# Two-stream DeepNorm backbone on one core: where the second half's scaling stands in ScalarE's queue

## The chip, the core and the metric

The kernel runs on one core of a Trainium2 chip. The metric is the device time of one execution in microseconds (us). The engines work side by side, each through its own queue in order: TensorE (PE in the rows, PEld for its weight loads), VectorE (DVE), ScalarE (ACT), GpSimd (POOL) and SyncE (SP), whose queue issues nearly all transfers here. An instruction at the head of a queue that waits for a semaphore holds up all that stands behind it in that queue.

## What is computed

Two layers run over 256 latent tokens (two row tiles of 128) with 1024 features; in the first layer 256 context tokens (two more row tiles) run through the same weights up to the attention. Each layer is a feed-forward block, a token mixer (attention in layer 0, a short gated convolution in layer 1) and a second feed-forward block. Each of these reads a modulated input and ends in a layer norm:

```python
def modulate(x, shift, scale):
    return x * (1 + scale) + shift

def post_norm_update(x, y, gate, res_w, g, b):
    return layer_norm(DN_ALPHA * x + res_w * gate * y, g, b)

def swiglu_ffn(h, w_in, w_out):
    a, u = jnp.split(h @ w_in, 2, axis=-1)
    return (jax.nn.silu(a) * u) @ w_out

def half_step_ffn(x, shift, scale, gate, w_in, w_out, g, b):
    y = swiglu_ffn(modulate(x, shift, scale), w_in, w_out)
    return post_norm_update(x, y, gate, 0.5, g, b)
```

## The kernel before

Every matmul is done in three parts on numbers split in two: `split` (L108) has ScalarE write a rounded "hi" copy (L110), and VectorE write the rest, "lo" = value - hi (L111). Weights are split in the same way as they come in: SyncE loads a raw tile (`wunit`, L203), ScalarE makes hi in two halves (L208), VectorE lo in two halves (L211). `mmu` then issues hi x hi (L162), lo x hi (L163) and hi x lo (L165). Four raw weight tiles exist, so a load is issued when the lo copies of the tile four loads earlier are through.

The function that the change touches is `modulated` (L408). It is called 12 times, once for each row tile at the end of each block that has a follower: four tiles after the first feed-forward block, and two tiles each after the attention, the second feed-forward block, the first block of layer 1 and the convolution. It normalizes the tile on VectorE (L411, which waits for a small GpSimd step, L400 and L401, behind the statistics of L398). Later it does for each half h of the 1024 features: four 128x128 transposes on TensorE into one PSUM bank (L419), four scalings of 128x128 on ScalarE that apply the modulation and the norm's gain (L425), then the hi copy (L110, tile hTh) and the lo copy (L111, tile hTl). The matmuls of the next block take the first half's hTh and hTl for their first two weight units (k = 0 to 3) and the second half's for the next two.

TensorE's order is written out by hand. For the other engines a scheduler lays out the order when the program is built: among the instructions that it reckons to be ready it takes them by priority, and `tc.high_priority` moves a block ahead. `queued(ins)` (L373) adds an order: instructions of the block come behind the given ones in the same engine's queue. A moved instruction on one engine can therefore change the order of others, SP's transfers among them.

Other names in the steps below: `roped` (L856 to L863) rotates queries and keys on VectorE, and L939 transposes the queries on TensorE; `gated` makes the gate (`sil`, L476 on ScalarE, L477 on VectorE), which TensorE transposes a little later (L485); `new_x` (L778, L779) multiplies x by the norm's gain `lng` and adds `lnb`, which SP loads just before (L343).

Of the kernel before, what the change touches and what calls it, by code (L numbers as in the profile page):

```python
# [11 lines left out]
AF = mybir.ActivationFunctionType  # L12
# [4 lines left out]
P = 128  # L17
# [51 lines left out]
def backbone_kernel(  # L69
# [6 lines left out]
    nc = tc.nc  # L76
# [16 lines left out]
    def nm(s):  # L93
        uid[0] += 1
        return f"{s}_{uid[0]}"

    def act(dt=F32, s="a"):
        return ap.tile([P, 512], dt, tag="act", name=nm(s))
# [7 lines left out]
    def tpb(s="tp"):  # L106
        return bank("tp", s)

    def split(src, hi, lo):
        a = nc.scalar.activation(hi, src, AF.Copy)  # L110
        return a, nc.vector.tensor_tensor(out=lo, in0=src, in1=hi.bitcast(F32), op=ALU.subtract)  # L111
# [261 lines left out]
    def queued(ins):  # L373

        es = ExitStack()
        for i in ins:
            es.enter_context(tc.issue_after(i.ins))
        return es
# [29 lines left out]
    def modulated(z, mv, rs, GB, lag, ahead=False):  # L408

        for h in range(2):  # L410
            norm_ins[1:] = [nc.vector.tensor_scalar(z[h], z[h], mv[:, 0:1], rs, op0=ALU.subtract, op1=ALU.mult)]  # L411

        def rest():
            G, B = GB.get()
            res = []
            for h in range(2):
                ps = tpb("hT")
                for k in range(4):
                    nc.tensor.transpose(ps[:, k * P:(k + 1) * P], z[h][:, k * P:(k + 1) * P], ident)  # L419
                t = sp.tile([P, 512], F32, tag="s2", bufs=S2, name=nm("h"))  # L420
                with tc.high_priority(offset=LN_EARLY):
                    hi, lo = act(F32R, "hTh"), act(F32R, "hTl")
                    for k in range(4):
                        s, c = slice(k * P, (k + 1) * P), slice(4 * h + k, 4 * h + k + 1)
                        nc.scalar.activation(t[:, s], ps[:, s], AF.Identity, bias=B[:, c], scale=G[:, c])  # L425
                    ins = split(t, hi, lo)
                res.append((hi, lo))
            if ahead:
                fence[:] = [i.ins for i in ins]
            return res  # L430

        return Late(lag, rest)
# [266 lines left out]
    for q, (k0, n) in enumerate(steps):  # L699
        nxt = start_step(*steps[q + 1]) if q < 4 else iter(())  # L700
        for g in range(6 * n):
            for _ in range(NS[min(q, 2)][g]):
                next(nxt, 0)
            k = k0 + g // 6
# [517 lines left out]
```

## Time and profile before

| | |
|---|---|
| median of 3 runs | 1264.56 us (1263.3 to 1265.16) |
| the profiled execution | 1262.04 us, of which the span of the core is 1260.2 us |
| granted TensorE clock | 0.999 of full speed |
| TensorE matmul busy | 1242.7 us, 99% of the span |
| TensorE weight loads busy | 1004.2 us, 80% |
| VectorE busy | 950.1 us, 75% |
| ScalarE busy | 589.2 us, 47% |
| GpSimd busy | 41.5 us, 3% |

Times in the trace are counted from the start of the span. The profiled execution took 1262.04 us, 2.5 us less than the median of the runs. In the rows of a timeline the first number is the start, the second the time from there to the end of the last instruction that is merged into the row, and a bracket at the end gives the idle time of that engine before the row and what ended it.

### The profile page before, as it was taken

The numbers are of one execution on the slowest core, as the hardware profiler recorded it, in microseconds if no ns is written. First come the engines' busy times: TensorE is split into PE (matmuls) and PEld (weight loads), VectorE is DVE, ScalarE is ACT, GpSimd is POOL, SyncE is SP. The second block draws the span as 40 slices with busy tenths as digits, with TensorE's granted clock in tenths as the row PEclk, the third lists the DMA queues.
The fourth block names the chain that finished last, engine by engine and source line by source line (L and its number), as shares of the span: only waits on it lengthen the run. The fifth ranks groups of instructions, "written<-read, shape, count | busy, mean of one in ns | idle before, by whom it ended". The sixth has DMA issues, their size and how long they took to land.

```text
span 1260.2 us, 17282 instructions
## 1 busy us (share of the span) xinstructions
PE 1242.7 (99%) x5910; PEld 1004.2 (80%) x5910; DVE 950.1 (75%) x1678; ACT 589.2 (47%) x1152; POOL 41.5 (3%) x71
## 2 busy tenths in 40 slices
PE   8999999999999999989999999999999999999997
PEld 5787778777878877867888788888788887888786
DVE  3699987888868877789889546988546788976546
ACT  2432132312326456687655435655435744655431
POOL 0000000000001111121000000000000000000000
PEclk9999999999999999999999999999999999999999
DMA  9976678788842744464899645898645764886641
GB/s 308 299 240 220 197 241 291 254 269 281 284 137 85 218 92 92 93 148 147 263 321 338 221 146 168 278 341 275 213 146 170 245 204 131 270 282 184 228 152 55
DMA packets 202776, 268.59 MB, mean 213 GB/s; under 512 B 30090, under 2 KB 149362, under 8 KB 202688
## 3 DMA queue, kind: packets, MB, share of 16 engines
q1 hardware_dynamic: 202652, 267.48, 67.2%
q8 instruction: 46, 0.75, 0.2%
q14 instruction: 42, 0.34, 0.1%
q10 hardware_dynamic: 36, 0.02, 0.0%
HBM read 265.27 MB, written 2.17 MB: 212 GB/s over the span
## 4 chain that ended last, share of the span: by engine, by line
PE 90%; ACT 3%; DVE 3%; DMA 2%; issue 1%; SPq 0%; POOL 0%; DVEq 0%; ACTq 0%
PE f L677 19%; PE w L162 17%; PE w L165 17%; PE w L163 17%; PE wkv L162 2%; PE wkv L163 2%; PE wkv L165 2%; PE wc L162 2%; PE wc L165 2%; PE wc L163 2%; PE gT L485 1%; DMA ar<-in_ada_w_dram 1%; PE ada L325 1%; PE hT L419 1%; PE S L962 1%
## 5 line engine op out<-in xcount | busy, mean ns | idle before, releaser
L208 ACT ACTIVATE w1h<-w1r 128x512 fp32r<-128x512 f32 (+1 forms) x352 | 199.9, 620 | 183.6 <-DMA w1r<-in_ffn_w_in_dram 63.5
L211 DVE TENSOR_TENSOR w1l<-w1r,w1h 128x512 fp32r<-128x512 f32 (+1 forms) x352 | 222.8, 678 | 49.2 <-ACT w1h L208 47.6
L162 PE MATMUL w<-w1h,hTh 128*128 128x512 f32 x528 | 209.4, 397 | 0.9 <-ACT hTh L110 0.9
L163 PE MATMUL w<-w1l,hTh 128*128 128x512 f32 x528 | 206.0, 390 | 0.2 <-DVE w1l L211 0.2
L294 DVE SCALAR_TENSOR_TENSOR acc<-ar,cst,acc 128x512 f32<-128x512 f32 x266 | 186.0, 745 | 14.5 <-DMA ar<-in_ada_w_dram 14.3
L162 PE MATMUL w<-w2h,gh 128*128 128x512 f32 (+1 forms) x446 | 173.4, 389 | 0.0
L163 PE MATMUL w<-w2l,gh 128*128 128x512 f32 (+1 forms) x446 | 172.1, 386 | 0.0
L211 DVE TENSOR_TENSOR w2l<-w2r,w2h 128x512 fp32r<-128x512 f32 x176 | 114.3, 687 | 76.3 <-ACT w2h L208 75.5
L208 ACT ACTIVATE w2h<-w2r 128x512 fp32r<-128x512 f32 x176 | 101.6, 624 | 145.4 <-PE w L165 101.6
L165 PE MATMUL w<-w1h,hTl 128*128 128x512 f32 x528 | 163.2, 390 | 0.3 <-DVE hTl L111 0.2
L165 PE MATMUL w<-w2h,gl 128*128 128x512 f32 (+1 forms) x446 | 136.0, 386 | 0.0
L677 PE MATMUL f<-h0h,w1h 128*128 128x512 f32 x352 | 132.8, 393 | 1.0 <-ACT w1h L208 0.6
L677 PE MATMUL f<-h0l,w1h 128*128 128x512 f32 x352 | 133.2, 391 | 0.0
L677 PE MATMUL f<-h0h,w1l 128*128 128x512 f32 x352 | 132.7, 390 | 0.0
L162 PEld LDWEIGHTS w<-w1h,hTh 128*128 128x128 f32 x528 | 99.2, 188 | 23.8 <-ACT hTh L110 1.7
L165 PEld LDWEIGHTS w<-w1h,hTl 128*128 128x128 f32 x528 | 98.9, 188 | 22.4 <-DVE hTl L111 1.5
L163 PEld LDWEIGHTS w<-w1l,hTh 128*128 128x128 f32 x528 | 99.2, 188 | 20.2 <-DVE w1l L211 0.6
L162 PEld LDWEIGHTS w<-w2h,gh 128*128 128x128 f32 x446 | 83.8, 188 | 19.3 <-issue 1.7
L163 PEld LDWEIGHTS w<-w2l,gh 128*128 128x128 f32 x446 | 83.8, 188 | 16.5
L165 PEld LDWEIGHTS w<-w2h,gl 128*128 128x128 f32 x446 | 83.3, 188 | 17.1
L677 PEld LDWEIGHTS f<-h0h,w1h 128*128 128x128 f32 x352 | 65.5, 188 | 19.4 <-issue 4.2
L677 PEld LDWEIGHTS f<-h0l,w1h 128*128 128x128 f32 x352 | 65.6, 188 | 14.3 <-issue 1.0
(184 smaller groups left out, 1697.3 us busy)
## 6 DMA issues: line engine op xcount, KB each, us to landing
w1r<-in_ffn_w_in_dram SPq DMA_DIRECT2D x340, 256.0 KB
ar<-in_ada_w_dram SPq DMA_DIRECT2D x128, 512.0 KB
w2r<-in_ffn_w_out_dram SPq DMA_DIRECT2D x88, 512.0 KB
ar<-in_ada_w_dram SPq DMA_DIRECT2D x32, 256.0 KB
wkvr<-in_na_w_qkv_dram SPq DMA_DIRECT2D x32, 256.0 KB
wcr<-in_sc_w_in_dram SPq DMA_DIRECT2D x32, 256.0 KB
wqr<-in_na_w_qkv_dram SPq DMA_DIRECT2D x8, 512.0 KB
bias<-in_na_rpb_dram SPq DMA_DIRECT2D x64, 64.0 KB
```

The costliest lines, as they stand in the source:

```text
L162: nc.tensor.matmul(ps, lh, rh, start=first and i == 0, stop=False)
L163: nc.tensor.matmul(ps, lh, rl, start=False, stop=False)
L165: nc.tensor.matmul(ps, ll, rh, start=False, stop=last and i == n - 1)
L208: nc.scalar.activation(hi[:, a:a + m // W_HI], raw[:, a:a + m // W_HI], AF.Copy)
L211: nc.vector.tensor_tensor(out=lo[:, a:b], in0=raw[:, a:b], in1=hi[:, a:b].bitcast(F32), op=ALU.subtract)
L294: nc.vector.scalar_tensor_tensor(out=a, in0=src, scalar=sc, in1=a, op0=ALU.mult, op1=ALU.add)
L325: nc.tensor.matmul(ps[32 * j:32 * j + 32, :], ones, acc[i][h], start=True, stop=True)
L419: nc.tensor.transpose(ps[:, k * P:(k + 1) * P], z[h][:, k * P:(k + 1) * P], ident)
L485: nc.tensor.transpose(ps[:, j * 256 + i * P:j * 256 + (i + 1) * P], g[:, j * P:(j + 1) * P], ident)
L677: nc.tensor.matmul(ps, w, hT0[k][part == 1], start=(k == part == 0), stop=(k == KC - 1 and part == 1))
L962: nc.tensor.matmul(banks[i], (qh, qh, ql)[f][ps, qs], (kh, kl, kh)[f][ps, :], start=f == 0, stop=f == 2)
```

## The change

In `modulated`, the four scalings of the second half (h = 1) are put behind the first half's hi copy (`ins[0]`) in ScalarE's queue. Nothing is added, removed or resized; no number changes.

```diff
                     hi, lo = act(F32R, "hTh"), act(F32R, "hTl")
-                    for k in range(4):
-                        s, c = slice(k * P, (k + 1) * P), slice(4 * h + k, 4 * h + k + 1)
-                        nc.scalar.activation(t[:, s], ps[:, s], AF.Identity, bias=B[:, c], scale=G[:, c])
+                    with queued([ins[0]] if h else ()):
+                        for k in range(4):
+                            s, c = slice(k * P, (k + 1) * P), slice(4 * h + k, 4 * h + k + 1)
+                            nc.scalar.activation(t[:, s], ps[:, s], AF.Identity, bias=B[:, c], scale=G[:, c])
                     ins = split(t, hi, lo)
```

In all 12 calls the order before is: four scalings of the first half, one of the second, hi copy of the first, three scalings of the second, hi copy of the second. TensorE's and GpSimd's orders stay as they are; ScalarE's changes in all 12 calls, and VectorE's and SP's around some of them. Line numbers of the changed kernel are one higher from L423 on.

**After the attention, first row tile.** ScalarE before, where `h_5702` and `h_5716` are the scaled halves, `hTh_5703` and `hTh_5717` their hi copies, and `w1h_5760` the hi copy of the third weight unit of the next block:

```order
L208 ACTIVATE w1h_5760<-w1r_5759 128x512
L425 ACTIVATE h_5702<-hT_5697,gcol_5490 128x128 x4
L425 ACTIVATE h_5716<-hT_5711,gcol_5490 128x128
L110 ACTIVATE hTh_5703<-h_5702 128x512
L425 ACTIVATE h_5716<-hT_5711,gcol_5490 128x128 x3
L208 ACTIVATE w1h_5760<-w1r_5759 128x512
L110 ACTIVATE hTh_5717<-h_5716 128x512
```

and ScalarE now:

```order
L208 ACTIVATE w1h_5760<-w1r_5759 128x512
L426 ACTIVATE h_5702<-hT_5697,gcol_5490 128x128 x4
L208 ACTIVATE w1h_5760<-w1r_5759 128x512
L110 ACTIVATE hTh_5703<-h_5702 128x512
L426 ACTIVATE h_5716<-hT_5711,gcol_5490 128x128 x4
L110 ACTIVATE hTh_5717<-h_5716 128x512
```

The place of the fifth scaling ahead of the first hi copy is taken by a weight copy of 128x512, which stood ahead of the second hi copy. (In the other calls nothing takes that place, except for the fourth tile of the first block and the second tile here, where it is a weight copy too.)

VectorE at the same place before, with `w1l_5761` and `w1l_5776` the lo copies of the third and fourth weight units, `st`, `mv` and `rs` the statistics of the second row tile:

```order
L111 TENSOR_TENSOR hTl_5704<-h_5702,hTh_5703 128x512
L389 SCALAR_TENSOR_TENSOR x_5241<-x_5241,res_5731 128x512
L211 TENSOR_TENSOR w1l_5776<-w1r_5774,w1h_5775 128x512
L111 TENSOR_TENSOR hTl_5718<-h_5716,hTh_5717 128x512
L391 BN_STATS st_5673<-x_5241 128x6
L211 TENSOR_TENSOR w1l_5761<-w1r_5759,w1h_5760 128x512
L398 BN_AGGR mv_5735<-st_5673 128x2
L211 TENSOR_TENSOR w1l_5776<-w1r_5774,w1h_5775 128x512
L411 TENSOR_SCALAR x_5239<-x_5239,mv_5735,rs_5737 128x512
L411 TENSOR_SCALAR x_5241<-x_5241,mv_5735,rs_5737 128x512
```

and VectorE now:

```order
L111 TENSOR_TENSOR hTl_5704<-h_5702,hTh_5703 128x512
L389 SCALAR_TENSOR_TENSOR x_5241<-x_5241,res_5731 128x512
L211 TENSOR_TENSOR w1l_5761<-w1r_5759,w1h_5760 128x512
L391 BN_STATS st_5673<-x_5241 128x6
L111 TENSOR_TENSOR hTl_5718<-h_5716,hTh_5717 128x512
L398 BN_AGGR mv_5735<-st_5673 128x2
L211 TENSOR_TENSOR w1l_5776<-w1r_5774,w1h_5775 128x512
L411 TENSOR_SCALAR x_5239<-x_5239,mv_5735,rs_5737 128x512
L411 TENSOR_SCALAR x_5241<-x_5241,mv_5735,rs_5737 128x512
L211 TENSOR_TENSOR w1l_5776<-w1r_5774,w1h_5775 128x512
```

The second half of `w1l_5761` moves ahead; the second half of `w1l_5776` moves behind the two L411, which wait for GpSimd.

**At the start of the attention.** VectorE before, with `qr_3652` the rotated queries of the second row tile (`r_621` its scratch) and `wkvl` the lo copies of key and value weights:

```order
L211 TENSOR_TENSOR wkvl_3709<-wkvr_3707,wkvh_3708 128x512
L111 TENSOR_TENSOR hTl_3619<-h_3617,hTh_3618 128x512
L856 TENSOR_TENSOR qr_3652<-wq_3599,rope 128x512
L861 TENSOR_TENSOR r_621_3653<-wq_3599,rope 128x16x16 x2
L111 TENSOR_TENSOR hTl_3633<-h_3631,hTh_3632 128x512
L863 TENSOR_TENSOR qr_3652<-qr_3652,r_621_3653 128x512
```

and VectorE now:

```order
L211 TENSOR_TENSOR wkvl_3709<-wkvr_3707,wkvh_3708 128x512 x2
L111 TENSOR_TENSOR hTl_3619<-h_3617,hTh_3618 128x512
L857 TENSOR_TENSOR qr_3652<-wq_3599,rope 128x512
L862 TENSOR_TENSOR r_621_3653<-wq_3599,rope 128x16x16 x2
L211 TENSOR_TENSOR wkvl_3724<-wkvr_3722,wkvh_3723 128x512
L864 TENSOR_TENSOR qr_3652<-qr_3652,r_621_3653 128x512
```

One more weight copy stands ahead of the row tile's rotation, and ahead of its last step there is a weight copy where `hTl_3633` stood.

**After the second feed-forward block of layer 0, second row tile.** VectorE before, with `w1l_7689` a lo copy of the next block's weights and `hTl_7553` the lo copy of the first half:

```order
L211 TENSOR_TENSOR w1l_7659<-w1r_7657,w1h_7658 128x512 x2
L211 TENSOR_TENSOR w1l_7689<-w1r_7687,w1h_7688 128x512 x2
L111 TENSOR_TENSOR hTl_7553<-h_7551,hTh_7552 128x512
L292 TENSOR_SCALAR acc_7622<-ar_7574,cst 128x512 x2
L111 TENSOR_TENSOR hTl_7567<-h_7565,hTh_7566 128x512
```

and VectorE now:

```order
L211 TENSOR_TENSOR w1l_7659<-w1r_7657,w1h_7658 128x512 x2
L211 TENSOR_TENSOR w1l_7689<-w1r_7687,w1h_7688 128x512
L111 TENSOR_TENSOR hTl_7553<-h_7551,hTh_7552 128x512
L211 TENSOR_TENSOR w1l_7689<-w1r_7687,w1h_7688 128x512
L292 TENSOR_SCALAR acc_7622<-ar_7574,cst 128x512 x2
L111 TENSOR_TENSOR hTl_7567<-h_7565,hTh_7566 128x512
```

`hTl_7553` now stands one weight copy earlier.

On SP some transfers change places. The one that the text below speaks of is in the second feed-forward block of layer 0: before, the four loads of `lng` and `lnb` for `new_x` stood ahead of the two loads of the weight tile `w1r_6151`; now the first of those two stands ahead of them. VectorE's order there has the first L778 (which needs `lng`) directly behind the gate of the first row tile and ahead of the gate of the second, before and now.

## Rows read from the trace of the kernel before

**Rows 1.** The page: busy time by engine, and the chain's shares by engine.
```profile
PE 1242.7 (99%) x5910; PEld 1004.2 (80%) x5910; DVE 950.1 (75%) x1678; ACT 589.2 (47%) x1152; POOL 41.5 (3%) x71
...
PE 90%; ACT 3%; DVE 3%; DMA 2%; issue 1%; SPq 0%; POOL 0%; DVEq 0%; ACTq 0%
```
**Rows 2.** Waits of PE, whole span: us in total, times, longest.
```profile
PE w L162 <- ACT hTh L110: 0.9, 2, 0.7
...
PE w L165 <- DVE hTl L111: 0.2, 1, 0.2
```
**Rows 3.** Timeline of ACT after the convolution, first row tile.
```profile
1062.83 1.85 ACT L425 ACTIVATE h<-hT,gcol 128x128 f32<-128x128 f32 x5 [2.01 <-PE hT L419]
1064.56 0.64 ACT L110 ACTIVATE hTh<-h 128x512 fp32r<-128x512 f32 x1
1065.08 1.17 ACT L425 ACTIVATE h<-hT,gcol 128x128 f32<-128x128 f32 x3
1066.28 0.63 ACT L110 ACTIVATE hTh<-h 128x512 fp32r<-128x512 f32 x1
```
**Rows 4.** Timelines of DVE and PE after the convolution, second row tile.
```profile
1074.70 0.68 DVE L111 TENSOR_TENSOR hTl<-h,hTh 128x512 fp32r<-128x512 f32 x1
...
1075.44 0.73 PE L165 MATMUL w<-w1h,hTl 128*128 128x512 f32 x2
```
**Rows 5.** Timeline of ACT after the attention, first row tile.
```profile
589.91 1.85 ACT L425 ACTIVATE h<-hT,gcol 128x128 f32<-128x128 f32 x5
591.63 0.65 ACT L110 ACTIVATE hTh<-h 128x512 fp32r<-128x512 f32 x1
```
**Rows 6.** Timeline of DVE at the same place.
```profile
592.86 0.67 DVE L111 TENSOR_TENSOR hTl<-h,hTh 128x512 fp32r<-128x512 f32 x1
...
596.47 0.19 DVE L398 BATCH_NORM_AGGREGATE mv<-st 128x2 f32<-128x12 f32 x1
...
597.93 1.00 DVE L411 TENSOR_SCALAR x<-x,mv,rs 128x512 f32<-128x512 f32 x2 [0.72 <-POOL rs L401]
598.85 1.28 DVE L211 TENSOR_TENSOR w1l<-w1r,w1h 128x512 fp32r<-128x512 f32 x2
```
**Rows 7.** Timeline of PE at the same place.
```profile
596.59 0.50 PE L163 MATMUL w<-w1l,hTh 128*128 128x512 f32 x1 [0.19 <-DVE w1l L211]
...
597.86 0.39 PE L162 MATMUL w<-w1h,hTh 128*128 128x512 f32 x1
598.08 0.39 PE L163 MATMUL w<-w1l,hTh 128*128 128x512 f32 x1
```
**Rows 8.** Timelines of DVE and PEld at the start of the attention.
```profile
412.03 0.69 DVE L863 TENSOR_TENSOR qr<-qr,r 128x512 f32<-128x512 f32 x1
...
412.77 0.75 PEld L939 LDWEIGHTS qT<-ident,qr 128*128 128x128 f32 x7 [0.32 <-DVE qr L863]
```
**Rows 9.** Timelines of DVE and PE after layer 0's second block, second row tile.
```profile
791.47 0.68 DVE L111 TENSOR_TENSOR hTl<-h,hTh 128x512 fp32r<-128x512 f32 x1
...
791.60 0.39 PE L163 MATMUL w<-w1l,hTh 128*128 128x512 f32 x1
792.21 0.73 PE L165 MATMUL w<-w1h,hTl 128*128 128x512 f32 x2 [0.21 <-DVE hTl L111]
```
**Rows 10.** Timelines of SP, DVE and PEld around `new_x`, layer 0, second block.
```profile
612.08 0.94 SPq L343 DMA_DIRECT2D lng<-in_ln_g_dram  x2
...
614.60 11.63 SPq L203 DMA_DIRECT2D w1r<-in_ffn_w_in_dram  x8
...
618.26 0.68 DVE L778 TENSOR_TENSOR x<-x,lng 128x512 f32<-128x512 f32 x1
...
620.35 0.58 PEld L485 LDWEIGHTS gT<-ident,sil 128*128 128x128 f32 x4
```
**Rows 11.** Timelines of SP and DVE around `new_x`, layer 1, first block.
```profile
801.49 0.93 SPq L343 DMA_DIRECT2D lng<-in_ln_g_dram  x2
...
807.47 1.29 DVE L778 TENSOR_TENSOR x<-x,lng 128x512 f32<-128x512 f32 x2 [1.21 <-DMA lng<-in_ln_g_dram]
```

## The prediction

> **What bounds the kernel now.** I read the page first, then TensorE's waits over the whole span, then the timelines of ScalarE, VectorE, TensorE and SyncE around each of the 12 calls of `modulated`. TensorE is busy 1242.7 of 1260.2 us and has 90% of the chain that ended last [rows 1]. All that TensorE does not do in the span is 17.5 us, so a change that leaves its work alone can gain only out of that. The change touches the hi copies of the modulated input, and for them TensorE waits 0.9 us in two places, and 0.2 us for a lo copy [rows 2]. The reader is to see there that the direct stake is about 1 us of 1260, and that whatever else the change does, it does through the order in which ScalarE, VectorE and SyncE now stand.
>
> The sum is made against the profiled execution: 1262.04 us with a span of 1260.2 us. The median of the runs shown is 1264.56 us, 2.52 us above; I add that difference at the end.
>
> **Part 1, the copy itself.** In a call the five scalings start 0.35 us apart: five of them take 1.85 us and one alone some 0.46 [rows 3]. The first hi copy starts 1.73 us after the first scaling, though its own four are through after 3 x 0.35 + 0.46 = 1.51 us. In the second half the copy starts 0.03 us after its last scaling has ended (1065.08 + 1.17 = 1066.25, copy at 1066.28) [rows 3]. So with nothing in between the first copy would start at about 1.54 us: 0.19 earlier. The second copy gets four scalings behind the first copy in place of three, so it comes 0.35 - 0.19 = 0.16 later. Nine of the 12 calls go this way. In the other three a weight copy slips into the gap, which takes 0.52 us of the queue (1064.56 to 1065.08 for a copy of that size [rows 3]) in place of 0.35, and the first hi copy comes 0.17 later.
>
> What that is worth at TensorE: the 0.7 us wait [rows 2] is the one after the convolution, where the first copy ends at 1065.20 [rows 3]. It would shrink by 0.19. But nine microseconds on, TensorE waits for the second row tile's lo copy, which VectorE ends at 1074.70 + 0.68 = 1075.38, with the matmul at 1075.44 [rows 4]; VectorE works without a gap up to there and starts nothing earlier. The 0.19 is lost again: 0, with 0 to -0.19 as bounds. The 0.2 us wait is the one after the attention. There a weight copy slips in, so the first copy starts at 589.91 + 4 x 0.35 + 0.52 = 591.82 instead of 591.63 [rows 5] and ends at 592.47. TensorE starts 0.19 later, but the first matmul with the lo half waits for VectorE, which reaches that copy at 592.86 as before [rows 6], so nothing is left of it: 0. The second halves are first needed two weight units later, 2.7 us at 12 matmuls of 0.22 to 0.23 us [rows 7]; a copy that is 0.16 later costs nothing.
>
> A rule of the Trainium skill speaks against this change: in the page Perfetto Trace Analysis, section "Optimizing Scalar/DVE Operations", half of a ScalarE instruction's profiled latency is write acknowledgement that overlaps with the next instruction, so an independent instruction between a producer and its reader is a cover, and the change removes one in each call. The trace agrees: the copy that stands directly behind its scaling starts 0.50 us after that scaling's start (1065.08 + 2 x 0.35 = 1065.78), where 0.35 would do [rows 3]. By the rows the exposed 0.15 us falls on ScalarE, busy 47% [rows 1], and is worth 0; by the rule alone, if all 12 lay on the path, the sum would have 12 x 0.15 = 1.8 us more (rival C).
>
> **Part 2, VectorE after the attention.** Here the scheduler now places the second half of the fourth weight unit's lo copy (`w1l_5776`) behind the two L411, which wait for GpSimd. VectorE's slots are 0.60 us (two in 1.28, one 0.68 [rows 6]). From the lo copy at 592.86: L389 593.46, `w1l_5761` 594.06, statistics 594.67, second lo copy 595.27, L398 at 595.87, which is one slot earlier than 596.47. From L398 to L411 it is 1.46 us [rows 6], so L411 starts at 597.33. The pair takes 0.92 (597.93 to 598.85 [rows 6]), so the delayed copy runs from 598.25 to 598.92. TensorE wants it at 598.08 [rows 7], and before that gets back the 0.35 us stall at 596.59, because `w1l_5761` is now early. It can start at about 598.98: **+0.90 us**. From there on every wait in the trace hangs on TensorE's own progress or has slack, so it stays. If GpSimd's step were 0.3 us faster it would be +0.6; that is the lower bound. The upper bound is +0.9, since the copy's time does not depend on TensorE.
>
> **Part 3, VectorE at the start of the attention.** The query transposes wait for the last step of the second row tile's rotation, L863 at 412.03, which ends at 412.72; the weight load goes at 412.77 after a wait of 0.32 [rows 8]. Now one weight copy more stands ahead of the rotation (the lo copy before it moves too, and some of VectorE's idle time there goes, so I reckon +0.5 us for its start), and ahead of L863 a weight copy replaces a lo copy of the same length. L863 comes at about 412.45: **+0.45 us**. Bounds 0.4 to 0.5 if it stays; attention has other waits of TensorE that could take it back, so the lower bound is 0.
>
> **Part 4, VectorE after layer 0's second block.** The lo copy at 791.47 holds TensorE: matmuls follow each other by 0.22 to 0.23 us, so after 791.60 the next was due at 791.83, started at 792.21, and its slot was 0.11 longer (0.73 in place of 0.62 for two) [rows 9]. The copy now stands one slot of 0.60 earlier and ends at 791.55: **-0.49 us**. Lower gain 0.2, if the gate a few microseconds on becomes the next wait.
>
> All else that moves in the queues (weight copies that trade places with gate copies, `lng` ahead of half a weight load) lies beside TensorE's work with several microseconds to spare: 0.
>
> **Sum.** 0 + 0.90 + 0.45 - 0.49 = +0.86 us: profiled 1262.9, span 1261.1, and with the 2.52 us of the median 1265.4 us. With the bounds of the parts: -0.19 + 0.6 + 0 - 0.49 = -0.1 to 0 + 0.9 + 0.5 - 0.2 = +1.2, 1264.5 to 1265.8. The runs of before lie 1.9 us apart, so a median may sit 0.9 us to either side.
>
> **Rival A, slower: `lng` comes late.** In layer 0's second block SyncE now issues one load of a weight tile ahead of `lng`. That load waits for a raw tile to come free, which was so at 614.60 [rows 10] and will be some 0.75 us later, as VectorE there runs later. `lng` is then issued at about 615.8 instead of 612.08. If it takes 5.9 us, as from 801.49 to about 807.4 [rows 11], it lands at 621.7. L778 stood at 618.26 without a wait, and behind it, 0.6 us on, the gate of the second row tile, which TensorE's transposes take from 620.35 [rows 10]. With the 0.9 us of part 2 TensorE comes at 621.25; the gate would be through at 621.7 + 0.6 + 0.4 = 622.7: a stall of 1.45 us. Against it: the loads issued ahead should have drained by then, and `lng` may land within 3 to 4 us. It decides from a landing after 620.3. With the parts at their upper bounds: 1.2 + 1.45 = +2.65, 1267.2 us, slower by 0.21%; with the forecast's parts 1266.9.
>
> **Rival B, the gains alone.** VectorE's new orders cost nothing (GpSimd's step or the scaling earlier than reckoned, or attention takes it back), and TensorE keeps the 0.19 and the 0.49: -0.7 us, 1263.9. For it: parts 2 and 3 rest on slots that I counted out, not on rows of the new order, and 0.9 us is less than two slots. Against it: at 598.08 TensorE has no slack that a copy behind L411 could use.
>
> **Rival C, the second copy sits on the path.** The rule of part 1: 12 x 0.15 = 1.8 us on top of the sum, +2.7 and 1267.2 us. Against it: the 2.7 us until the second half is needed.
>
> **How the numbers follow.** Forecast 0.62, A 0.18, B 0.16, C 0.04. 0.2% is 2.5 us, about what a measurement of this kernel can tell from no change: faster means under 1262.0, slower over 1267.1. Forecast and its spread lie inside but for 0.02; B gives 0.03 to faster, of A half is over the bound, of C half (0.02). That is faster 0.03, same 0.84, slower 0.13. The range takes the forecast with the scatter of the median (1264.5 - 0.9), B for the most part and A: 1263.4 to 1267.2.
>
> **What would show it.** Right: in the changed profile the first hi copy 1.54 us after the first scaling in nine calls; TensorE's L163 waiting about 1.2 us for a `w1l` near 597 to 600 and no stall before it; the query transposes waiting 0.7 to 0.8 us for L864; no wait for `hTl` near 792. Wrong: a wait of TensorE for the gate near 621 (A), no new wait after the attention (B), a wait for the second half's hTh (C), or a new wait in the attention that the order does not show.

## The result and the profile after

The changed kernel took 1266.95 us in the median of 9 runs (1265.67 to 1268.93) beside 1263.97 us for the kernel before in its 9 runs: a ratio of 1.0025 with a 95% interval of 1.0017 to 1.0033, so +3.0 us (+2.1 to +4.2). Predicted were 1265.4 us, in the range of 1263.4 to 1267.2, and +0.86 us. Measured a second time (e5 below), it was +1.9 us (ratio 1.0015, 1.0006 to 1.0025). The profiled execution of after took 1267.37 us with a span of 1265.5 us, 5.3 us more than that of before.

The page of after, for [rows 1]: busy times, TensorE's own row in the 40 slices with the granted clock (PEclk, tenths of full speed; 9 is 90% or more), and the chain by engine.

```profile
PE 1247.3 (99%) x5910; PEld 1008.3 (80%) x5910; DVE 950.5 (75%) x1678; ACT 591.6 (47%) x1152; POOL 41.5 (3%) x71
...
PE   8999999999999999989999999999999999999997
...
PEclk9999999999999999989999999999999999999999
...
PE 87%; DVE 6%; ACT 2%; DMA 2%; issue 1%; POOL 1%; SPq 0%; DVEq 0%; ACTq 0%; POOLq 0%
```

The same 5910 matmuls keep TensorE busy 4.6 us longer, and in one slice, near 555 us, the clock shows an 8. TensorE's waits over the whole span (total us, times, longest), for [rows 2]:

```profile
PE w L163 <- DVE w1l L211: 1.2, 1, 1.2
PE w L162 <- ACT hTh L110: 0.9, 2, 0.5
...
PE qT L940 <- DVE qr L864: 0.3, 1, 0.3
```

The wait for `w1l` is new, as foretold in part 2; the one for `qr` as in part 3; that for `hTl` (part 4) is gone, and none for a gate stands in the list (rival A).

TensorE's order is the same in every kernel of this study but for added matmuls, so the start of each matmul can be set against that of its twin in the profiled execution of before. The difference is how far a kernel has fallen behind by then; where it grows, time is lost. By stretches of the time before:

| stretch, us of before | after falls behind by | what lies there |
|---|---|---|
| 0 to 60 | +0.86 | first loads, clock still at its lower level |
| 60 to 395 | 0.00 | |
| 395 to 420 | +0.36 | start of the attention (part 3) |
| 420 to 545 | +0.83 | attention (+0.41 near 437 us; +0.33 near 516 us, where e1 below loses as much) |
| 545 to 585 | +2.84 | end of the attention, lower clock |
| 585 to 610 | +1.00 | behind the attention (part 2) |
| 610 to 780 | -0.06 | (rival A would stand here) |
| 780 to 800 | -0.51 | layer 0, second block (part 4) |
| 800 to the end | 0.00 | convolution (part 1) included |

The three steps of the forecast are there, +0.36, +1.00 and -0.51, together +0.85 us. Most of the rest is one stretch of 10 us in which nothing was foretold. Stretches of before and of after there, TensorE alone (length, busy us with the matmuls that start in it, granted clock, DMA share, GB/s); the kernel before first:

```profile
550.00:553.00 3.00, 2.25 (x13) 1.00 0.77 106
553.00:556.00 3.00, 3.00 (x18) 1.00 0.75 181
556.00:560.00 4.00, 4.00 (x28) 1.00 1.05 378
```

and after:

```profile
550.00:553.00 3.00, 1.03 (x7) 0.95 0.85 195
553.00:556.00 3.00, 3.00 (x11) 0.50 0.60 77
556.00:560.00 4.00, 4.00 (x14) 0.56 0.75 257
```

TensorE looks fully busy in either, but after gets 25 matmuls done from 553 to 560 us where before did 46: the clock stands at 0.50, the lower of the chip's two levels (1.2 GHz instead of 2.4). The timeline of TensorE in after shows what the engine did before it fell, and when it rose:

```profile
549.57 0.60 PE L988 MATMUL PT<-ident,pr 128*128 128x128 f32 x4
550.58 0.66 PE L922 MATMUL kT<-ident,kr 128*128 128x128 f32 x4 [0.42 <-DVE pT L111]
552.80 1.12 PE L922 MATMUL kT<-ident,kr 128*128 128x128 f32 x4 [1.56 <-DVE pT L111]
...
556.04 0.63 PE L163 MATMUL wo<-wol,oT 128*128 128x512 f32 x1
556.47 0.63 PE L162 MATMUL wo<-woh,oT 128*128 128x512 f32 x1
...
559.71 0.40 PE L162 MATMUL wo<-woh,oT 128*128 128x512 f32 x1
559.94 0.40 PE L163 MATMUL wo<-wol,oT 128*128 128x512 f32 x1
```

It stood still for 0.42 and then for 1.56 us, because `pT` kept the bank that the transposes need; then the products follow each other 0.43 us apart, and from 559.5 us again 0.23. The same two waits are in the trace of before, with the same lengths:

```profile
548.53 0.66 PE L921 MATMUL kT<-ident,kr 128*128 128x128 f32 x4 [0.42 <-DVE pT L111]
550.75 0.66 PE L921 MATMUL kT<-ident,kr 128*128 128x128 f32 x4 [1.56 <-DVE pT L111]
```

There the clock stayed up. So the question for the experiments is whether the change brings the clock down, or whether that happens to the kernel before as well and its one profiled execution escaped it.

### The profile page after: what moved, and what is told of

Same layout as the page of the kernel before. It is cut to its first block, busy times and chain, and to the rows that moved or that the text cites. A ratio compares the mean times of both kernels' runs of the same rounds, so it can differ in the third digit from the quotient of the medians.

```text
span 1265.5 us, 17284 instructions
## 1 busy us (share of the span) xinstructions
PE 1247.3 (99%) x5910; PEld 1008.3 (80%) x5910; DVE 950.5 (75%) x1678; ACT 591.6 (47%) x1152; POOL 41.5 (3%) x71
## 4 chain that ended last, share of the span: by engine, by line
PE 87%; DVE 6%; ACT 2%; DMA 2%; issue 1%; POOL 1%; SPq 0%; DVEq 0%; ACTq 0%; POOLq 0%
PE f L678 18%; PE w L162 17%; PE w L165 17%; PE w L163 17%; PE wkv L162 2%; PE wc L162 2%; PE wc L165 2%; PE wc L163 2%; DMA ar<-in_ada_w_dram 2%; PE wkv L163 2%; PE wkv L165 2%; PE gT L486 1%; PE S L963 1%; PE ada L325 1%; PE PT L988 1%
## 5 line engine op out<-in xcount | busy, mean ns | idle before, releaser
L163 PE MATMUL w<-w1l,hTh 128*128 128x512 f32 x528 | 206.0, 390 | 1.2 <-DVE w1l L211 1.2
L163 PE MATMUL w<-w2l,gh 128*128 128x512 f32 (+1 forms) x446 | 172.1, 386 | 0.0
L163 PEld LDWEIGHTS w<-w1l,hTh 128*128 128x128 f32 x528 | 99.3, 188 | 21.1 <-DVE w1l L211 1.7
L163 PEld LDWEIGHTS w<-w2l,gh 128*128 128x128 f32 x446 | 83.8, 188 | 16.6
```

The source lines that it names most:

```text
L163: nc.tensor.matmul(ps, lh, rl, start=False, stop=False)
```

## The experiments

All were timed in turn with the kernel before, on the same chip within a group: e1 to e4, e5 to e8, e9 to e11, and e12 alone. The calls of `modulated` are counted by a list that grows by one in each call:

```diff
-            G, B = GB.get()
+            G, B = GB.get(); ncall.append(0)
...
-                    with queued([ins[0]] if h else ()):
+                    with queued([ins[0]] if h and CALLS else ()):
```

CALLS is `len(ncall) != 4` in e2, `len(ncall) != 5` in e3, `len(ncall) in (1, 3, 7, 8, 9, 10, 11)` in e4, e7, e11 and e12, `len(ncall) in (4, 5)` in e6, `len(ncall) in (1, 3, 7, 9, 10, 11)` in e8, `False` in e9 and `True` in e10. e1 is before with an empty line, so that its line numbers are those of after, and e5 is after itself. e7 and e9 to e12 have a further edit, shown below.

> The kernel before, unchanged in what it does (one empty line), so that the granted clock of each of its runs is on show and not only that of its one profiled execution (0.999). Aligned matmul by matmul, the profiled execution of after falls behind that of before by 0.87 us up to 27 us, by a further 1.1 us between 412 and 518 us, by 2.9 us between 550.9 and 558 us, where after's matmuls run at a granted clock of 0.50, and by 0.5 us in all behind that. Theory A, the fall of the clock near 553 us belongs to the change: nearly all runs here have a mean granted clock of 0.998 to 0.999, median time 1262.0 to 1264.5 us. Theory B, it happens to either kernel and the profiled execution of before was one that escaped it: most runs here have 0.996 to 0.997, as all nine of after have, and the runs at 0.999 are some 3 us faster than the others.

> The change in all calls but the fourth (the second tile of context in layer 0's first block, just ahead of the attention), which goes back to the order of before. By the aligned traces that call costs 1.1 us: 0.39 us at the first query transpose (412.8 us of before) and 0.24, 0.1 and 0.33 us at three later places of the attention where the matmuls wait for kTl and qTl. Theory A (the clock falls near 553 us because of the changed order at the start of the attention): 1.1 + 2.9 = 4.0 us less than after, about 1263.0 us, granted clock 0.999. Theory B (the clock falls in either kernel): 1.1 us less than after, about 1265.9 us, granted clock 0.996 to 0.997.

> The change in all calls but the fifth (first tile behind the attention, 590 us), which goes back to the order of before: the second half of w1l_5776 is again computed ahead of the two normalizations. Predicted for that order was +0.90 us; the aligned traces show +0.91 us between 592 and 604 us (+0.20, -0.19, -0.37, +1.27). Expected: 0.9 us less than after, about 1266.0 us, with no wait of the product with w1l near 600 us and the short wait for w1h (0.2 to 0.4 us) in its place. Neither theory of the clock has this call, 40 us behind the fall, change the clock: 0.996 to 0.997 as in after. If the clock is at 0.999 here, what decides it is nothing that this order does.

> The change in seven calls alone: 1, 3, 7, 9, 10, 11, where nothing but the hi copy of ScalarE changes its place, and 8, the second tile of layer 0's second block, where the lo copy hTl_7553 stands a slot earlier on VectorE. Predicted for the eighth: -0.49 us; the aligned traces show -0.34 us at 792 us, and a further -0.3 us at 1065 us behind the convolution. Up to the attention's end it is the kernel before. Expected against before: -0.3 to -0.8 us in fixed terms. Theory A: granted clock 0.999 and 1263.2 to 1263.7 us; theory B: the same mixture of clocks as in the kernel before itself, and times that differ by it.

What the four measured, and the later kernels beside them. Times are medians; the stretches are those of the table above, of the one profiled execution of each; "clock" is the mean granted clock of that execution:

| kernel | against before, us (95%) | 0-60 | 395-420 | 420-545 | 545-585 | 585-610 | 780-800 | clock |
|---|---|---|---|---|---|---|---|---|
| after | +3.0 (+2.1 to +4.2) | +0.86 | +0.36 | +0.83 | +2.84 | +1.00 | -0.51 | 0.996 |
| e1 before again | +0.9 (-0.3 to +2.0) | +0.07 | 0.00 | +0.43 | +3.20 | 0.00 | 0.00 | 0.995 |
| e2 all but the 4th | +0.9 (-0.4 to +1.9) | 0.00 | -0.03 | +1.07 | +1.48 | +1.03 | -0.49 | 0.997 |
| e3 all but the 5th | +0.2 (-0.8 to +1.4) | -1.12 | +0.39 | +0.21 | +1.51 | +0.01 | -0.49 | 0.998 |
| e4 seven calls | -0.1 (-1.3 to +1.0) | +0.39 | -0.03 | +0.54 | +3.39 | +0.01 | -0.49 | 0.995 |
| e5 after again | +1.9 (+0.8 to +3.2) | -0.01 | +0.35 | +0.34 | +0.04 | +0.99 | -0.52 | 0.999 |
| e6 4 and 5 alone | +2.5 (+1.1 to +3.3) | +0.36 | +0.23 | +0.47 | +3.45 | +1.02 | -0.02 | 0.996 |
| e7 work in the gap | +0.1 (-1.0 to +1.1) | -0.68 | -0.01 | -0.02 | +1.55 | +0.01 | -0.52 | 0.999 |
| e8 hi copy alone | +0.7 (-0.1 to +2.0) | +0.03 | +0.01 | -0.02 | +1.72 | 0.00 | -0.01 | 0.997 |
| e9 before, filled | -0.3 (-1.9 to +0.3) | +0.26 | +0.01 | -0.05 | +0.08 | 0.00 | +0.01 | 0.998 |
| e10 after, filled | 0.0 (-1.0 to +1.3) | -0.49 | +0.37 | +1.55 | -0.02 | +0.99 | -0.49 | 0.998 |
| e11 seven calls, filled | -1.7 (-2.9 to -0.6) | -0.03 | 0.00 | +0.62 | -0.06 | 0.00 | -0.51 | 0.998 |
| e12 the same again | -1.2 (-2.8 to -0.5) | +1.14 | -0.01 | +0.35 | +1.17 | -0.02 | -0.50 | 0.999 |

**e1, the kernel before again.** The clock fell there too; stretches of TensorE in e1:

```profile
550.00:553.00 3.00, 1.63 (x8) 0.82 0.85 146
553.00:556.00 3.00, 3.00 (x9) 0.50 0.50 100
556.00:560.00 4.00, 4.00 (x18) 0.66 0.94 324
```

From 545 to 585 us this execution of the kernel before lost 3.20 us against the one that I had read. Theory A, as I had put it (nearly all runs of before at 0.998 to 0.999), is out: of the 110 runs of before in the four groups, 68 had a granted clock of 0.997 or less, 36 were at 0.998 and 6 at 0.999. In the first group the 20 runs at 0.997 took 1264.2 us on average and the 3 at 0.999 1262.75, so the expected 3 us between them is 1.5. The profiled execution of before, at 0.999 and 1262.04 us, is one that escaped. The mean clock of an execution is a rough sign only: that of e3, at 0.998, has the fall in it.

**e2 and e3, one call taken back.** Without the fourth call the step of +0.36 at 395 to 420 us goes, and the fall of the clock stays (+1.48): that call doesn't make it. Without the fifth the step of +1.00 goes, and so does TensorE's wait. Its waits from 585 to 610 us in e3 show the shorter wait of before in its place:

```profile
PE hT L419 <- DVE x L411: 0.4, 2, 0.2
PE w L162 <- ACT hTh L110: 0.2, 1, 0.2
PE w L163 <- DVE w1l L211: 0.2, 1, 0.2
```

Both medians came out below after's first one by more than their step, 2.0 and 2.8 us; against its second (e5) it is 1.0 and 1.7 us, so part of that is scatter. In e2 I expected 1263.0 by theory A and 1265.9 by B, and it is 1264.9, between them.

**e4, seven calls.** The eighth call's -0.49 us is there to the hundredth; the median is 0.1 us under that of before (-1.3 to +1.0). Of a further -0.3 us at 1065 us, which I had expected from the first two traces, there is -0.21, and it is given back at 1075 us, as part 1 had it: from 800 us to the end all of these kernels stand within 0.05 us.

> The changed kernel itself, beside the others of this group. Aligned traces of the first five runs give fixed terms that came out alike in every kernel that has the call in question: the fourth call +0.36 to +0.39 us between 395 and 420 us, the fifth +1.00 to +1.03 us between 585 and 610 us, the eighth -0.49 to -0.51 us between 780 and 800 us, sum +0.88 us. Everything else (the first 60 us, the attention from 420 to 545 us, the fall of the clock near 552 us) also differs between two executions of the kernel before. Theory B1, the change is worth its fixed terms alone: +0.9 us against before, and the +2.98 us measured first is this plus some 2 us of such variation; here then 0 to +2 us, with a mixture of granted clocks like that of before. Theory B2, the change also makes the fall of the clock more likely or longer: +3 us again and no run above 0.997.

> The two calls that cost, alone. Fixed terms +0.37 and +1.01 us, so +1.4 us against before (theory B1), in the trace as these two steps at 395 to 420 and 585 to 610 us and no step at 780 to 800 us. By theory B2, which has the fourth call's order bring the clock down, +3.4 us.

> The seven calls of e4 and, at the end of the attention, the first four transposes of the last kT done three times over into the same bank (the first two passes are overwritten), so that TensorE has 0.9 us of work in the wait of 1.55 us for pT that stands just ahead of the fall of the clock; on ScalarE and VectorE three or four neighbouring instructions change places behind it. If the clock falls because TensorE stands still there, nearly all runs have a granted clock of 0.998 to 0.999 (only the last microseconds and the start are slow) and the time is 1.5 to 3 us less than that of e4: about 1261 to 1262.5 us. If the fall has nothing to do with that wait, the clocks are the mixture seen so far (0.995 to 0.999) and the time is that of e4, or up to 1 us more by the added work.

> The change in the six calls in which it moves nothing but the hi copy on ScalarE (1, 3, 7, 9, 10, 11). Predicted for these: 0 on the path, at most -0.19 us behind the convolution. So the time of before within 0.3 us by the fixed terms; what is measured beyond that is how far two programs of the same instructions stand apart. A rival, that the completion of the first half's four scalings is paid for twice when the copy stands right behind them, would make it 6 x 0.15 = 0.9 us slower.

**e5, after again.** In this profiled execution of the same program the clock did not fall, and it took 1263.2 us, 4.2 less than the first; its steps are +0.35, +0.99 and -0.52. Its 12 runs fall into two groups: four at 0.998 or 0.999 took 1262.9 to 1264.3 us, eight at 0.996 or 0.997 took 1265.4 to 1268.6. B2 had put no run of it above 0.997, and that is refuted; but the median is +1.9 us, at the upper end of what B1 allowed.

**e6, the costly calls alone.** The two steps are there (+0.23 and +1.02, for the +0.37 and +1.01 expected) and the one at 780 us is not; TensorE's waits from 770 to 810 us are again those of [rows 2]:

```profile
PE w L165 <- DVE hTl L111: 0.2, 1, 0.2
```

The median, +2.5 us, lies between B1 (+1.4) and B2 (+3.4), and its interval (+1.1 to +3.3) holds the first alone.

**e8, the hi copy alone.** All three steps are 0, so the rule of the rival in its expectation, 0.15 us a call on the path, costs nothing here; the median is +0.7 us with 0 in the interval. The clock fell here as well, but elsewhere. Stretches of TensorE in e8:

```profile
540.00:545.00 5.00, 3.68 (x24) 1.00 0.54 124
545.00:550.00 5.00, 5.00 (x29) 0.66 0.69 124
550.00:553.00 3.00, 1.39 (x9) 1.00 0.81 108
```

Here it went down behind the pair of waits for `pT` at 543.2 and 544.2 us (0.76 and 0.56 us), and was up again when the longer wait came. Of its 1.72 us from 545 to 585, 0.94 is the fall less what the longer wait gave back; the other 0.8 us comes between 556 and 570 us, at a granted clock of 1.00, so this stretch of the table holds more than the clock. So in the ten microseconds from 543 to 553 there are two places at which the clock may go down.

**e7, work in the gap.** It is e4 with the transposes of the first half of the last pair of `kT` (g = 3, j = 0) done three times over:

```diff
-                for t in range(4):
-                    nc.tensor.transpose(ps[:, t * P:(t + 1) * P], krs[t][:, j * P:(j + 1) * P], ident)
+                for t in range(4 * (1 + 2 * (g == 3 and j == 0))):
+                    nc.tensor.transpose(ps[:, t % 4 * P:(t % 4 + 1) * P], krs[t % 4][:, j * P:(j + 1) * P], ident)
```

The profiled execution kept its clock, and 9 of 11 runs are at 0.998 or 0.999. But it still lost 1.55 us from 545 to 585, and the median of 1264.2 us misses the 1261 to 1262.5 expected. The scheduler had put a weight copy ahead of the lo copy `kTl` on VectorE, and TensorE now waits for that. TensorE's waits from 540 to 590 us in e7:

```profile
PE o L1001 <- DVE pT L111: 1.5, 3, 0.6
PE kT L922 <- DVE pT L111: 1.1, 2, 0.7
PE S L963 <- DVE kTl L111: 0.8, 1, 0.8
```

The clock stayed up, and the new order took the gain back. So for e9 to e12 I looked for a filling that leaves every other instruction in its place: five products ahead of the values of the head with h = 8 (the ninth; the expectations call it the eighth), which wait 0.75 us for `pT` at 543.2 us of before, and two ahead of the last pair of `kT`.

```diff
-                for t in range(4):
-                    nc.tensor.transpose(ps[:, t * P:(t + 1) * P], krs[t][:, j * P:(j + 1) * P], ident)
+                for t in range(2 * (g == 3 and j == 0)): nc.tensor.matmul(ps[:, 0:512], Q[1].get()[0][0][:, 0:P], Q[1].get()[0][0][:, 0:512], start=True, stop=True)
+                for t in range(4): nc.tensor.transpose(ps[:, t * P:(t + 1) * P], krs[t][:, j * P:(j + 1) * P], ident)
...
-        v = KV[h // 4][1]
+        v = KV[h // 4][1]; [nc.tensor.matmul(ps, v[0][:, s], v[0][:, 0:256], start=True, stop=True) for k in range({8: 5}.get(h, 0))]
```

> The kernel before with seven matmuls of no use, which leave every other instruction of every engine in its place: five products of v, 128x256, into the bank of the eighth head's values ahead of its first product (there TensorE waits 0.73 us for pT at 543.7 us) and two of qTh, 128x512, into the bank of the last kT ahead of its transposes (there the second half waits 1.55 us for pT at 551.2 us). Both banks are written over by the first real product. By the durations of the neighbours they are 5 x 0.12 and 2 x 0.22 us, 1.0 us in all, and lie in those waits. If the clock falls because TensorE stands still there: nearly all runs at 0.998 to 0.999, and 1 to 2 us less than before. If not: the clocks of before (0.996 to 0.999) and its time.

> The same seven matmuls in the changed kernel. Theory B1 (the change is worth its fixed terms, +0.36, +1.00 and -0.50 us, and what it measured beyond them is the clock's chance): 0.9 us more than e9, and clocks like those of e9. Theory B2 (something else in the change costs 1 to 2 us more): still 2 us or more above e9, at like clocks.

> The same seven matmuls in the kernel of e4, whose only fixed term is the eighth call's -0.49 us. Expected 0.5 us less than e9, so 1.5 to 2.5 us less than before where the filling holds the clock: then faster than both kernels. If the filling does nothing: the time of e4.

> The kernel of e11 once more, on whatever chip comes up, because 1.7 us is little beside the spread of single executions (1262.1 to 1266.9 us for the kernel before). If the filling holds the clock and the eighth call is worth its 0.49 us: again nearly all runs at 0.998 to 0.999 and 1 to 2 us less than before. If e11 was a lucky draw: within 0.5 us of before, although the clocks are as high as in e11.

The timeline of TensorE in e9 around the two places; L998 and L921 are the added products:

```profile
542.42 0.83 PE L998 MATMUL o<-v 128*128 128x256 f32 x5
543.42 0.38 PE L1000 MATMUL o<-pT,v 128*128 128x256 f32 x1 [0.17 <-ACT pT L110]
...
548.74 0.73 PE L921 MATMUL kT<-qTh 128*128 128x512 f32 x2 [0.40 <-DVE pT L111]
549.32 0.60 PE L922 MATMUL kT<-ident,kr 128*128 128x128 f32 x4
550.96 0.66 PE L922 MATMUL kT<-ident,kr 128*128 128x128 f32 x4 [1.04 <-DVE pT L111]
```

The waits of 0.75 and 1.56 us are down to 0.17 and 1.04, and the real matmuls behind them start within 0.1 us of where they did. In the 44 runs of e9 to e12 one is at 0.997, 24 are at 0.998 and 19 at 0.999. All four profiled executions kept their clock, and the share of runs at 0.999 rose from 6 of 110 to 19 of 44. That the standstill brings the clock down is shown by this: every engine's order in e9 is that of the kernel before but for the seven products. Which of the two places matters more was not tried apart, except that e7 fills the second alone.

What it brought in time is less than I had expected. e9 is 0.3 us faster than before, with 0 in the interval, where 1 to 2 were expected, so a gain of the filling by itself is not shown; e10 is level with before; e11 is 1.7 us faster (ratio 0.9986, 0.9977 to 0.9995) and e12, the same kernel on another chip, 1.2 us (0.9987, 0.9978 to 0.9996). e11 is **faster than before**, and so than after with its +1.9 and +3.0. More than the filling's 0.3 us and the eighth call's 0.49 is not accounted for. (The +1.17 us of e12 from 545 to 585 is no fall of the clock, which is 1.00 there: 0.5 us is a wait for `kTl` near 552 us, 0.6 us comes near 568 us.) Between kernels with the same filling, where the clock no longer scatters, the medians differ by +0.3 us (e10 against e9; +0.6 in the means; fixed steps +0.87) and +1.7 us (e10 against e11; fixed steps +1.4); e9 against e11 differ by 1.4 us, where the step is 0.5. With the clock held, the change is worth its steps within this scatter, as B1 says, and nothing of the 2 us or more that B2 asks for is left.

## Why the prediction was right and wrong

**Part 1, the copy itself: right.** ScalarE in after, behind the convolution, for [rows 3]:

```profile
1068.14 1.51 ACT L426 ACTIVATE h<-hT,gcol 128x128 f32<-128x128 f32 x4 [2.01 <-PE hT L419]
1069.68 0.63 ACT L110 ACTIVATE hTh<-h 128x512 fp32r<-128x512 f32 x1
```

The copy starts 1.54 us after the first scaling, as worked out, and TensorE's longest wait for `hTh` shrank from 0.7 to 0.5 us. Its matmuls are 0.20 us ahead from 1065 us on, for 0.19 foretold, and at 1075 us, at the lo copy of the second row tile, this is lost again (+0.01 over 1063 to 1085 us).

**Part 2, behind the attention: right.** VectorE in after, for [rows 6], with the delayed half of `w1l_5776` at the start of the last DVE row, and TensorE, for [rows 7]:

```profile
600.75 0.20 DVE L398 BATCH_NORM_AGGREGATE mv<-st 128x2 f32<-128x12 f32 x1
600.87 0.63 DVE L211 TENSOR_TENSOR w1l<-w1r,w1h 128x512 fp32r<-128x512 f32 x1
602.22 1.00 DVE L411 TENSOR_SCALAR x<-x,mv,rs 128x512 f32<-128x512 f32 x2 [0.71 <-POOL rs L401]
603.14 2.49 DVE L211 TENSOR_TENSOR w1l<-w1r,w1h 128x512 fp32r<-128x512 f32 x4
...
601.12 0.39 PE L163 MATMUL w<-w1l,hTh 128*128 128x512 f32 x1
...
603.88 0.50 PE L163 MATMUL w<-w1l,hTh 128*128 128x512 f32 x1 [1.24 <-DVE w1l L211]
```

From L398 to L411 it is 1.47 us as before, the copy runs behind the two L411, and TensorE waits 1.24 us for it while the earlier stall is gone. Predicted +0.90, measured +0.99 to +1.03 in each of the five profiled executions with this call.

**Part 3, the start of the attention: right in its place, a move missed behind it.** The weight load of the query transposes waits 0.71 us, in after:

```profile
414.02 0.75 PEld L940 LDWEIGHTS qT<-ident,qr 128*128 128x128 f32 x7 [0.71 <-DVE qr L864]
```

Predicted 0.7 to 0.8 and +0.45 us; measured +0.23 to +0.39. (By the prediction's own figures it is 412.45 - 412.03 = 0.42, and the copy of part 1 starts at 591.83, not 591.82; neither changes an outcome.) The +0.5 us for the rotation's start was a guess, a little high. But in the last step ahead of the sum, all other moves in the queues were set to 0, "with several microseconds to spare", and one had none: with the fourth call SyncE issues one weight load (two transfers) more ahead of `lng`, and some bias loads behind weight loads that stood behind them. SyncE and VectorE's wait for `lng` (420 to 520 us), before and then after:

```profile
418.06 1.49 SPq L343 DMA_DIRECT2D lng<-in_ln_g_dram  x2
...
DVE x L778 <- DMA lng<-in_ln_g_dram: 4.8, 1, 4.8
```

```profile
415.58 1.58 SPq L203 DMA_DIRECT2D wkvr<-in_na_w_qkv_dram  x2
417.77 2.07 SPq L875 DMA_DIRECT2D bias<-in_na_rpb_dram  x3
419.89 1.92 SPq L343 DMA_DIRECT2D lng<-in_ln_g_dram  x2
...
DVE x L779 <- DMA lng<-in_ln_g_dram: 6.0, 1, 6.0
```

Measured from TensorE's own progress up to 395 us, `lng` goes out 0.9 to 1.5 us later in the five profiled executions with the fourth call, and VectorE waits for it 5.9 to 6.4 us there, against 4.3 to 5.5 in the nine others. All that stands behind it on VectorE, `kTl` among it, comes later, and TensorE waits for `kTl` near 437 us: +0.2 to +0.8 us (0.4 on average) with the call. Without it the same place shows 0 to +0.74 (0.2 on average over the nine). So it is rival A's mechanism, but at another `new_x`. That `lng` comes later is shown; what it costs TensorE is perhaps 0.2 us, a difference of averages whose ranges overlap. At the place that I had named, VectorE waited 0.3 us for `lng` and TensorE not at all: rival A as put did not happen.

**Part 4, layer 0's second block: right.** Predicted -0.49, measured -0.49 to -0.52 in the nine profiled executions with this call; `hTl` starts 0.73 us ahead of the last L163 that TensorE does before it needs it, where before it was 0.13. In after, for [rows 9]:

```profile
796.70 0.68 DVE L111 TENSOR_TENSOR hTl<-h,hTh 128x512 fp32r<-128x512 f32 x1
...
797.43 0.39 PE L163 MATMUL w<-w1l,hTh 128*128 128x512 f32 x1
797.65 0.61 PE L165 MATMUL w<-w1h,hTl 128*128 128x512 f32 x2
```

**The sum and the step that failed.** +0.85 us in the profile for +0.86 predicted, and then +3.0 and +1.9 us in the two measurements, over the bound of 0.2% in the one and under it in the other. What failed is the step from the profile to the median: one profiled execution, at a clock of 0.999, was taken for the kernel's usual course, and its distance to the median, 2.52 us, for a constant that any kernel carries. Reckoned from the same profile, that distance is 4.05 us in after (1266.95 - 1262.9). That the median still lies in the range, 0.25 us under its end of 1267.2, is luck: that end came from rival A's stall of 1.45 us, which did not happen.

The distance was a warning. Part of it is the fall of the clock, which many runs had and that execution had not: the 6 runs of before at 0.999 took 1262.9 us on average, the 56 at 0.997 1264.1. Seven of the nine profiled executions without a filling have the fall (it cost 1.5 us in three of them and 2.8 to 3.5 in four), and no rival of mine named it.

How the +3.0 us divides can't be settled. The fixed steps are 0.85, and the later `lng` perhaps 0.2. The rest shows only in runs with a low clock: in e5's group the runs at 0.998 or 0.999 took 1263.6 us (after, 4 runs, too few to show even the 0.85) and 1263.5 us (before, 17 runs) on average, the runs at 0.996 or 0.997 took 1266.9 (after, 8) and 1264.1 (before, 18). Of the 32 runs of after, e5 and e6 11 are at 0.996 or lower, of the 110 of before 12. But the mean clock alone does not account for it: at the same 0.997 after took 1266.5 us (6 runs, first measurement) and 1266.7 (5 runs, e5), before 1264.1. A fall that cost 3 us where before's cost 1.5 would make most of that difference, but after has only two traces, one with such a fall and one with none, and before's program, e1, shows one of 3.2 us too. With the filling, which takes the falls away, the difference is back to +0.3 to +0.6 us (e10 against e9). That the part beyond the steps hangs on the standstill and the clock is therefore supported, not shown, and why the fall should be longer or more frequent in after is open. It isn't the fourth call alone, as theory B2 had it in e6: of the 11 runs of e3, which has it, only one is under 0.997.

One more reading is left. e1 and e8, which have none of the steps, stand 0.9 and 0.7 us above before, each with 0 in its interval, and beyond their steps e5 and e6 stand 1.0 and 1.2 us above it, known to about 1 us. So part of the rest may have nothing to do with the change; what else it would be is open too.

**Rivals B and C.** B fell with the wait of 1.24 us. C's rule would have cost 1.8 us over 12 calls; e8, with six of them and nothing else, shows no step at any of them that lasts.

## What to carry to other kernels

An order that the scheduler changes can be costed from the trace of before to one or two tenths of a microsecond, as the three steps here were, if each moved instruction's slot is counted out and each queue is followed, SyncE's to the next load that someone waits for. The profile that this rests on is one execution: where it stands 2.5 us from the median, first find out what the other runs have that it has not, from their granted clocks. Where a short standstill of TensorE brings its clock down, as here, a few products of no use in that wait can hold it up, so long as they push no instruction of another engine into a worse place; what that saves in time has to be measured, and here it was 0.3 us, not clear of 0.

## What the runs showed of the hardware

- A standstill of TensorE of 0.4 and 1.55 us, 0.6 us of work apart (in e8 of 0.76 and 0.56 us), brought the granted clock from 1.00 to 0.50 in some executions of the same program and not in others (after and e5); the fall cost 1.5 to 3.5 us. The Trainium skill (TensorE: Matmul & The Clock Gate, Part 1: The HAM clock gate) says that the clock has two levels and is set by how busy the array has been recently; the traces agree with both (0.50 and 1.00, and no fall in the five profiled executions with a filling).
- A fall does not show in TensorE's busy share: from 553 to 560 us both kernels are busy throughout, with 25 and 46 matmuls.
- Two programs with the same instructions (e1 and before) measured 0.9 us apart in the median over 11 and 33 runs, with an interval of -0.3 to +2.0.
